# Block 1's inputs, modulated once by side jobs, kept in DRAM and loaded straight into the tiles of their low parts

## The chip, the cores and the metric

The kernel runs on one core of one Trainium2 chip. The core has five engines with a queue of instructions each: TensorE (PE) multiplies matrices and adds into banks (PSUM tiles, named `ps`), ScalarE (ACT) and VectorE (DVE) work on whole tiles, GpSimd (POOL) and SyncE (SP) here do little but issue DMA transfers, which sixteen DMA engines carry out. An engine takes its queue in order; an instruction that waits holds all behind it. The metric is device microseconds (us) from start to end; several runs are timed, and one more execution is recorded by the hardware profiler.

## The reference

One decoder layer on 2048 tokens of width 1024, all in float32. Cut to what matters:

```python
mod = (silu(c) @ w_ada + b_ada)
sh1, sc1, g1, sh2, sc2, g2 = split(mod, 6)
h = x * (1 + sc1) + sh1                          # the modulated input
z = h @ w_in                                     # 1024 -> 2048 columns
gate_b, gate_c, v_conv, v_pool = split(z, 4)
y_conv = gate_b * causal_conv3(gate_c * v_conv)
y_pool = (trailing means over 2, 4, 8, 16 tokens - v_pool) @ w_pool * pool_scale
mix = concat(y_conv, y_pool) @ w_out
x = layer_norm(alpha * x + (1 + g1) * mix)
h = x * (1 + sc2) + sh2
f = square(relu(h @ w_mlp_in)) @ w_mlp_out       # 1024 -> 4096 -> 1024
x = layer_norm(alpha * x + (1 + g2) * f)
```

## The kernel before

**Numbers in two parts.** TensorE multiplies a short form of float32 (`fp32r`). To keep float32's accuracy every operand is cut in two: a high part (ScalarE's cast, L146) and a low part, what the cast lost (VectorE's subtraction, L147). `mm3` (L153 to L155) then issues three matmuls, high by high, high by low, low by high. Weights' parts lie in `w` tiles (6 of them), inputs' parts in `h` tiles (28), what is loaded and not yet cut in `r` tiles (5), intermediate results in `o` tiles (10). Each is 128 x 1024 numbers, 512 KB. A new name for a tile of a kind takes the place of an old one, and the first writer of the new one waits for the last reader of the old.

**Seven products.** The large matrix products are done by Winograd's scheme, two by two blocks with seven products in place of eight. Of the operands some blocks are raw, others sums of blocks. One product (`seven`) has two banks of 12 matmuls, 24 in all; behind its matmuls the code cuts the weights that come next.

**Stages.** Tokens go in two blocks of 1024. Block 0: input projection, output projection and layer norm, then the first MLP matrix (`first_map`) in eight groups `up(b, g)` of 512 hidden columns. Then the same for block 1, and at the end the second MLP matrix for both (`down`). In a group `keep` copies a product's banks into an `o` tile (ScalarE, L1086), `add` adds a product to such a tile, `squared` makes relu and square (ScalarE, L1098 and L1099), and `sums` adds and subtracts quarters of tiles on VectorE, in place, and stores them by POOL's queue into the DRAM tile `usum`. P0 to P6 below are the seven products of block 0's last group, g = 7.

**The turn.** In that group, behind P4, `turn()` calls `prepare()`: it loads what block 1's first input projection needs. The weights `wins` come raw (W0, W1) or summed (from the DRAM tile `winsum`; the first is S below). Inputs are needed raw, that is modulated (key "11" and "21"), or as one of seven sums of blocks (key "2", "1" and on), two tiles each. `summed_weights` loads weights through SyncE's queue (L624). `inputs` loads inputs, also by SyncE (L705): a summed one from the DRAM tile `xsum`, which is then cut by `split`; a raw one from the kernel's input `xT`, whereupon ScalarE modulates it twice, half a tile at a time, once into the `h` tile of the high part and once in place (four instructions of L712 for each tile), and VectorE subtracts for the low part. A program that puts each engine's instructions in order moves all this among P2 to P6 and their sums: the order the engines see is that of the rows shown below, not that of the code.

**Side jobs.** The sums in `xsum` and `winsum` are made earlier. `first_map` calls `beside` behind the products of groups 1 to 7 (a group has seven such calls, one for each product; beats 1 to 5 fall in group 1, 6 to 12 in group 2 and so on, 41 to 47 in group 7). `timed` starts a job at its beat and goes on with it three beats later. `sum_x(k)`, four of them, loads two tiles of `xT` by POOL's queue into two `o` tiles, modulates them (ScalarE), adds and subtracts in place (VectorE) and stores to `xsum`. `sum_first(p)`, two of them, does so with halves of `wins` for `winsum`. POOL's queue has a third kind of traffic: transfers that add w2's blocks to each other in DRAM (`wsum`, L1194), one behind each matmul triple whose number stands in `W_BEATS`.

## Time and profile before

| | |
|---|---|
| median of 3 runs | 1705.73 us (1704.62 to 1708.85) |
| the profiled execution | 1707.25 us |
| its span, first to last instruction | 1705.5 us |
| granted TensorE clock, mean | 0.997 of full speed |
| TensorE busy | 99% of the span |
| VectorE, ScalarE, POOL busy | 82%, 49%, 22% |

The profile is one execution. Its rows name an engine, a line of the code, the operation, and `out<-in` by the tiles' names without their numbers; "x" is a count. A row with square brackets at the end tells how long the engine stood idle before the instruction, and whose end it waited for. In rows of transfers the last figures are sizes and the time from issue to landing. In rows that begin with two times and a colon (a stretch of the span) stand, in this order, its length and the busy us (with the number of instructions) of TensorE, of its weight loads, of VectorE, ScalarE and POOL, then the granted clock, the share of DMA engines' time in use, and GB/s. Groups 1 to 7 of block 0 run from about 313 to 577 us, some 38 us each.

### The profile page before, as it was taken

What the parts mean: (1) busy time and instruction counts of PE and PEld (TensorE: products, weight loads), DVE (VectorE), ACT (ScalarE), POOL (GpSimd) and SP (SyncE); (2) the same over time, 40 slices, a digit from 0 to 9 for tenths busy, and PEclk for the clock granted to TensorE, in tenths of its full rate; (3) what the DMA queues carried; (4) which work ended last, traced back from release to release, by engine and by line L of the source; (5) the groups of instructions that cost most, each with busy time, mean ns of one, the idle gap of its engine ahead of it and who ended that gap; (6) DMA issues with size and microseconds to landing.
All of it is one profiled execution on the core that took longest, in us unless ns stands there. A gap on an engine that the chain in (4) does not pass through costs nothing.

```text
span 1705.5 us, 22025 instructions
## 1 busy us (share of the span) xinstructions
PE 1688.1 (99%) x7519; PEld 1396.8 (82%) x7519; DVE 1399.6 (82%) x2138; ACT 844.2 (49%) x1160; POOL 377.9 (22%) x687
## 2 busy tenths in 40 slices
PE   9999999999999899999999999999999999999998
PEld 7888888888888688888888888888888888888886
DVE  8898697888887586886888788766988887897898
ACT  6323358555554753345855454445543433334555
POOL 0222221445564122200145455430000000000000
PEclk9999999999999999999999999999999999999999
DMA  9998877668778778865889998899899999896782
GB/s 387 346 335 323 312 253 275 224 218 259 241 247 221 228 234 223 238 241 197 267 251 266 243 244 243 240 330 355 317 344 338 384 328 353 292 338 222 264 291 99
DMA packets 149217, 469.47 MB, mean 275 GB/s; under 512 B 20456, under 2 KB 20976, under 8 KB 149104
## 3 DMA queue, kind: packets, MB, share of 16 engines
q1 hardware_dynamic: 93184, 303.38, 50.5%
q0 software_dynamic: 55920, 164.67, 32.0%
q8 instruction: 59, 0.97, 0.3%
q14 instruction: 54, 0.44, 0.1%
HBM read 350.01 MB, written 159.91 MB: 299 GB/s over the span
## 4 chain that ended last, share of the span: by engine, by line
PE 90%; DVE 4%; DMA 3%; ACT 1%; issue 1%; POOL 0%; DVEq 0%; SPq 0%; ACTq 0%; POOLq 0%
PE ps L153 29%; PE ps L155 29%; PE ps L154 29%; PE ps L488 3%; DVE o L164 2%; DMA r<-in_xT 1%; PE ps L865 1%; DMA usum<-o 1%; DVE w L147 1%; DMA w<-in_w 1%; DVE r L164 0%; DMA wsum<-in_w 0%; DMA r<-in_w 0%; POOL usum L1111 0%; ACT w L146 0%
## 5 line engine op out<-in xcount | busy, mean ns | idle before, releaser
L153 PE MATMUL ps<-h,w 128*128 128x512 f32 x1312 | 511.9, 391 | 5.9 <-ACT w L146 4.2
L155 PE MATMUL ps<-h,w 128*128 128x512 f32 x1312 | 511.3, 390 | 0.5 <-DVE w L147 0.5
L154 PE MATMUL ps<-h,w 128*128 128x512 f32 x1312 | 511.7, 390 | 0.0
L153 PE MATMUL ps<-h,h 128*128 128x512 f32 (+1 forms) x1064 | 412.4, 388 | 0.9 <-DVE h L164 0.9
L154 PE MATMUL ps<-h,h 128*128 128x512 f32 (+1 forms) x1064 | 412.4, 388 | 0.9 <-DVE h L147 0.9
L155 PE MATMUL ps<-h,h 128*128 128x512 f32 (+1 forms) x1064 | 412.4, 388 | 0.0
L153 PEld LDWEIGHTS ps<-h,w 128*128 128x128 f32 x1312 | 246.9, 188 | 58.5 <-ACT w L146 4.7
L155 PEld LDWEIGHTS ps<-h,w 128*128 128x128 f32 x1312 | 246.7, 188 | 53.3 <-DVE w L147 1.7
L154 PEld LDWEIGHTS ps<-h,w 128*128 128x128 f32 x1312 | 247.1, 188 | 51.3
L1111 POOL DMA_DIRECT2D usum<-o x416 | 225.2, 550 | 254.2 <-DVE o L164 162.6
L146 ACT CAST w<-r 128x1024 fp32r<-128x1024 f32 x156 | 164.2, 1052 | 196.0 <-PE ps L154 190.4
L147 DVE TENSOR_TENSOR w<-r,w 128x1024 fp32r<-128x1024 f32 x156 | 190.6, 1223 | 59.9 <-ACT w L146 59.1
L146 ACT CAST h<-r 128x1024 fp32r<-128x1024 f32 (+1 forms) x136 | 136.5, 1009 | 198.6 <-PE ps L154 79.6
L154 PEld LDWEIGHTS ps<-h,h 128*128 128x128 f32 x1064 | 199.8, 188 | 42.1 <-DVE h L147 1.3
L153 PEld LDWEIGHTS ps<-h,h 128*128 128x128 f32 x1064 | 199.8, 188 | 42.0 <-DVE h L164 1.1
L155 PEld LDWEIGHTS ps<-h,h 128*128 128x128 f32 x1064 | 199.8, 188 | 40.9
L164 DVE TENSOR_TENSOR o<-o,o 128x256 f32<-128x256 f32 (+2 forms) x458 | 200.7, 491 | 2.7 <-ACT o L1099 1.1
L147 DVE TENSOR_TENSOR h<-r,h 128x1024 fp32r<-128x1024 f32 (+1 forms) x136 | 157.8, 1168 | 51.2 <-ACT h L146 51.0
L146 ACT CAST h<-w 128x1024 fp32r<-128x1024 f32 x104 | 109.1, 1049 | 104.9 <-DVE w L164 95.1
L147 DVE TENSOR_TENSOR h<-w,h 128x1024 fp32r<-128x1024 f32 x104 | 127.1, 1222 | 14.9 <-ACT h L146 14.7
L164 DVE TENSOR_TENSOR o<-o,ps 128x512 f32<-128x512 f32 x184 | 122.7, 684 | 19.2 <-PE ps L155 17.3
L164 DVE TENSOR_TENSOR o<-o 128x256 f32<-128x256 f32 (+1 forms) x176 | 82.6, 472 | 25.3 <-ACT o L1099 14.9
(166 smaller groups left out, 1424.7 us busy)
## 6 DMA issues: line engine op xcount, KB each, us to landing
usum<-o POOLq DMA_DIRECT2D x416, 128.0 KB, 5.2
r<-usum SPq DMA_DIRECT2D x104, 512.0 KB, 5.5
w<-wsum SPq DMA_DIRECT2D x76, 512.0 KB, 7.3
w<-in_w SPq DMA_DIRECT2D x72, 512.0 KB, 7.1
r<-in_w SPq DMA_DIRECT2D x68, 512.0 KB, 7.0
wsum<-in_w POOLq DMA_DIRECT2D x56, 512.0 KB, 7.6
wsum<-wsum POOLq DMA_DIRECT2D x24, 512.0 KB, 5.5
msum<-o POOLq DMA_DIRECT2D x18, 512.0 KB, 6.5
```

Of the source, the lines that this page charges most:

```text
L146: high = nc.scalar.copy(hi, src)
L147: return high.ins, nc.vector.tensor_tensor(lo, src, hi.bitcast(F32), op=ALU.subtract).ins
L153: nc.tensor.matmul(ps, whi, xhi, start=first, stop=False, skip_group_check=goes_on)
L154: nc.tensor.matmul(ps, whi, xlo, start=False, stop=False, skip_group_check=goes_on)
L155: done = nc.tensor.matmul(ps, wlo, xhi, start=False, stop=last, skip_group_check=goes_on)
L164: return nc.vector.tensor_tensor(out_, a, b_, op=op)
L488: nc.tensor.matmul(ps[m, h], wt[:, w : w + P], A[k][p // 2][:, hs], start=k == 0 and p == 0, stop=k == KD - 1 and p == 2)
L865: nc.tensor.transpose(ps[:, t * P : t * P + P], R[4 * h + t][:, k * P : k * P + P], ident)
L1111: nc.gpsimd.dma_start(usum[slot, g // 2, :, b, g % 2, :], z)
```

## The change

There is a new DRAM tile, `xmod`. `sum_x` now stores its two modulated tiles there before it adds in place; it then stops once more, and adds two beats later. So a job holds its two `o` tiles two beats longer. The six jobs start at other beats: 4, 11, 18, 25, 32 and 39 in place of 5, 11, 13, 18, 20 and 26.

`inputs` loads all inputs, raw and summed, from `xmod` or `xsum` without an `r` tile: into the `h` tile of the low part, read as plain float32. `split` then casts from it to the high part, and VectorE subtracts in place. The modulations at L712 are gone: for each raw tile, four modulations of half a tile become one cast of a whole tile.

`inputs` also leaves its last load in the list `fed`, and the next load in `summed_weights` takes it from there: that load is issued behind it (`issue_after` sets an order on the queue, it waits for no data).

```diff
+    xmod = tc.dram_tile([KD, P, T], F32, name="xmod")
...
+    fed = []
+
     def summed_weights(src, sums, order):
         for i in order:
             r = t_r()
-            nc.sync.dma_start(r, src[i] if i in RAW else sums[i - 4])
+            with tc.issue_after(fed.pop()) if fed else nullcontext():
+                nc.sync.dma_start(r, src[i] if i in RAW else sums[i - 4])
             yield r
...
         for i, r in zip((k, k + 4), rs):
             nc.scalar.activation(r, r, AF.Identity, bias=mod[:, 2 * i + SH1 : 2 * i + SH1 + 1],
                                  scale=mod[:, 2 * i + SC1 : 2 * i + SC1 + 1])
+            nc.gpsimd.dma_start(xmod[i], r)
+        yield
         (b11, b12), (b21, b22) = ((r[:, :H], r[:, H:]) for r in rs)
...
         for q in range(2):
-            r = t_r()
             X[key, q] = hi, lo = t_h(), t_h()
...
-                src = xT
-            nc.sync.dma_start(r.rearrange("p (a n) -> p a n", a=2),
-                              src[k : k + 2, :, hs].rearrange("a p n -> p a n"))
-            if len(key) == 1:
-                split(r, hi, lo)
-                continue
-            for dst in (hi, r):
-                for a, cs in enumerate(halves):
-                    nc.scalar.activation(dst[:, cs], r[:, cs], AF.Identity,
-                                         bias=mod[:, 2 * (k + a) + SH1 : 2 * (k + a) + SH1 + 1],
-                                         scale=mod[:, 2 * (k + a) + SC1 : 2 * (k + a) + SC1 + 1])
-            tt(lo, r, hi.bitcast(F32), ALU.subtract)
+                src = xmod
+            r = lo.bitcast(F32)
+            fed[:] = [nc.sync.dma_start(r.rearrange("p (a n) -> p a n", a=2),
+                                        src[k : k + 2, :, hs].rearrange("a p n -> p a n")).ins]
+            split(r, hi, lo)
...
-            for _ in due.pop(beat, ()):
-                pass
+            for job in due.pop(beat, ()):
+                for _ in job:
+                    due.setdefault(beat + 2, []).append(job)
+                    break
             if beat in jobs:
                 next(jobs[beat])
-                due[beat + 3] = jobs[beat]
+                due.setdefault(beat + 3, []).append(jobs[beat])
...
-        return timed(dict(zip((5, 11, 13, 18, 20, 26), sums)))
+        return timed(dict(zip((4, 11, 18, 25, 32, 39), sums)))
```

What the engines see at the turn. In the rows, a name's first number is the tile's own; L624 has become L628, L705 has become L711, L1086 is L1084, L1098 and L1099 are L1096 and L1097. First SyncE's queue before; the row ahead of these is the load of P6's weights (r_657).

```order
L624 DMA r_682_4964<-in_wins 128x1024
L705 DMA r_685_4970<-in_xT 128x2x512
L705 DMA r_688_4979<-in_xT 128x2x512
L705 DMA r_691_4988<-in_xT 128x2x512
L705 DMA r_694_4997<-in_xT 128x2x512
L624 DMA r_697_5006<-in_wins 128x1024
L705 DMA r_700_5012<-xsum_147 128x2x512
L705 DMA r_703_5018<-xsum_147 128x2x512
L624 DMA r_713_5112<-winsum_145 128x1024
```

The weights W0, four raw inputs, the weights W1, two summed inputs, and the first summed weights. Now:

```order
L711 DMA h_686_4980<-xmod_147 128x2x512
L628 DMA r_682_4973<-in_wins 128x1024
L711 DMA h_688_4985<-xmod_147 128x2x512
L711 DMA h_690_4990<-xmod_147 128x2x512
L711 DMA h_692_4995<-xmod_147 128x2x512
L628 DMA r_693_4999<-in_wins 128x1024
L711 DMA h_697_5006<-xsum_148 128x2x512
L711 DMA h_699_5011<-xsum_148 128x2x512
L628 DMA r_707_5103<-winsum_145 128x1024
L711 DMA h_711_5136<-xsum_148 128x2x512
L711 DMA h_713_5141<-xsum_148 128x2x512
```

These loads are called A (h_686), W0 (r_682), B (h_688), C (h_690), D (h_692), W1 (r_693), E (h_697), F (h_699), S (r_707), G (h_711) and H (h_713). A now stands ahead of W0, and the tiles that A to H write were low parts of block 0's inputs: each waits for TensorE's last matmul with the old one. S's `r` tile held the weights of P4 (r_656).

ScalarE in the same place, before. w_676 is the high part of P4's weights, w_679 that of P5's, w_683 that of W0; o_673 takes P2's banks (the copies that free them for P4), o_678 takes P3's, o_664 is P0 and P1's result.

```order
L146 CAST w_676_4911<-r_656_4763 128x1024
L712 ACTIVATE h_686_4971<-r_685_4970,mod_94 128x512
L1098 ACTIVATE o_664_4804<-o_664_4804 128x1024
L712 ACTIVATE h_686_4971<-r_685_4970,mod_94 128x512
L1099 ACTIVATE o_664_4804<-o_664_4804 128x1024
L712 ACTIVATE r_685_4970<-r_685_4970,mod_94 128x512
L1086 COPY o_673_4882<-ps_660_4773 128x512
L146 CAST w_679_4942<-r_655_4762 128x1024
L1086 COPY o_673_4882<-ps_661_4787 128x512
L712 ACTIVATE r_685_4970<-r_685_4970,mod_94 128x512
L712 ACTIVATE h_689_4980<-r_688_4979,mod_94 128x512
L1086 COPY o_678_4915<-ps_674_4885 128x512
```

Two tiles are modulated among the copies, half by half. Now:

```order
L146 CAST h_685_4979<-h_686_4980 128x1024
L146 CAST h_687_4984<-h_688_4985 128x1024
L146 CAST w_676_4920<-r_656_4764 128x1024
L1096 ACTIVATE o_664_4805<-o_664_4805 128x1024
L1097 ACTIVATE o_664_4805<-o_664_4805 128x1024
L146 CAST h_689_4989<-h_690_4990 128x1024
L1084 COPY o_673_4891<-ps_660_4774 128x512
L146 CAST w_679_4951<-r_655_4763 128x1024
L1084 COPY o_673_4891<-ps_661_4788 128x512
L146 CAST h_691_4994<-h_692_4995 128x1024
L1084 COPY o_678_4924<-ps_674_4894 128x512
```

The casts of A and B stand ahead of w_676, that of C ahead of P2's first copy, that of D between the copies.

Then ScalarE up to P6's weights (r_657), before:

```order
L712 ACTIVATE h_692_4989<-r_691_4988,mod_94 128x512 x2
L712 ACTIVATE r_691_4988<-r_691_4988,mod_94 128x512 x2
L712 ACTIVATE h_695_4998<-r_694_4997,mod_94 128x512 x2
L712 ACTIVATE r_694_4997<-r_694_4997,mod_94 128x512
L1098 ACTIVATE o_678_4915<-o_678_4915 128x1024
L712 ACTIVATE r_694_4997<-r_694_4997,mod_94 128x512
L1099 ACTIVATE o_678_4915<-o_678_4915 128x1024
L146 CAST w_698_5008<-r_697_5006 128x1024
L146 CAST h_701_5013<-r_700_5012 128x1024
L146 CAST w_706_5048<-r_657_4764 128x1024
```

and now:

```order
L146 CAST h_696_5005<-h_697_5006 128x1024
L1084 COPY o_678_4924<-ps_675_4907 128x512
L146 CAST w_683_4975<-r_682_4973 128x1024
L146 CAST h_698_5010<-h_699_5011 128x1024
L146 CAST w_694_5001<-r_693_4999 128x1024
L146 CAST h_710_5135<-h_711_5136 128x1024
L1096 ACTIVATE o_678_4924<-o_678_4924 128x1024
L1097 ACTIVATE o_678_4924<-o_678_4924 128x1024
L146 CAST h_712_5140<-h_713_5141 128x1024
L146 CAST w_700_5039<-r_657_4765 128x1024
```

Between W0's cast and P6's (w_706 before, w_700 now) lay eight modulations of half a tile, P3's relu and square, and the casts of W1 and of E; now lie there the casts of F, W1, G and H and the same relu and square, with E's two rows ahead of W0's.

VectorE ahead of the low part of P6's weights, before (the last row):

```order
L147 TENSOR_TENSOR w_699_5009<-r_697_5006,w_698_5008 128x1024
L164 TENSOR_TENSOR o_681_4956<-o_681_4956,o_664_4804 128x256
L164 TENSOR_TENSOR o_681_4956<-o_681_4956,o_678_4915 128x256
L147 TENSOR_TENSOR h_702_5014<-r_700_5012,h_701_5013 128x1024
L147 TENSOR_TENSOR h_705_5020<-r_703_5018,h_704_5019 128x1024
L147 TENSOR_TENSOR w_707_5049<-r_657_4764,w_706_5048 128x1024
```

and now:

```order
L147 TENSOR_TENSOR h_711_5136<-h_711_5136,h_710_5135 128x1024
L164 TENSOR_TENSOR o_673_4891<-o_673_4891,ps_674_4894 128x512
L164 TENSOR_TENSOR o_678_4924<-o_678_4924 128x256
L164 TENSOR_TENSOR o_670_4848<-o_670_4848,o_678_4924 128x256
L164 TENSOR_TENSOR o_670_4848<-o_678_4924,o_664_4805 128x256
L164 TENSOR_TENSOR o_681_4965<-o_664_4805,o_678_4924 128x256
L164 TENSOR_TENSOR o_681_4965<-o_678_4924 128x256
L147 TENSOR_TENSOR h_713_5141<-h_713_5141,h_712_5140 128x1024
L164 TENSOR_TENSOR o_681_4965<-o_681_4965,o_664_4805 128x256
L164 TENSOR_TENSOR o_681_4965<-o_681_4965,o_678_4924 128x256
L147 TENSOR_TENSOR w_701_5040<-r_657_4765,w_700_5039 128x1024
```

The five rows of quarters (128x256) from o_678, which need P3's square, and two more that follow them, stood on both sides of W1's low part (w_699), five ahead of it and outside these rows; now all seven stand behind G's low part and W1's (w_695), with H's among them. P6's low part comes last in both.

TensorE mixes P6's matmuls with those of the input projection's first product, which needs W0, A and B alone. Before, it came to P6's high part after 9 matmuls of that product and to its low part 19 matmuls later; now it comes to the high part after 5 and to the low part 9 later.

## The prediction

> **What bounds the kernel now.** I read the page's head first, then what TensorE waited for, then the stretch round its longest wait engine by engine.
>
> ```profile
> span 1705.5 us, 22025 instructions
> PE 1688.1 (99%) x7519; PEld 1396.8 (82%) x7519; DVE 1399.6 (82%) x2138; ACT 844.2 (49%) x1160; POOL 377.9 (22%) x687
> ...
> PE ps L153 <- ACT w L146: 4.2, 1, 4.2
> PE ps L153 <- ACT o L1086: 1.7, 1, 1.7
> ...
> 560.00:570.00 10.00, 8.35 (x37) 6.53 (x37) 3.91 (x6) 10.00 (x15) 2.13 (x4) 1.00 0.35 107
> 570.00:580.00 10.00, 7.61 (x34) 5.98 (x32) 7.13 (x10) 9.88 (x14) 0.10 (x1) 1.00 0.69 215
> 580.00:590.00 10.00, 8.16 (x24) 6.55 (x25) 7.44 (x11) 4.50 (x5) 3.10 (x6) 0.66 0.93 284
> ```
>
> TensorE is busy for 99% of the span; its two long waits, both on ScalarE, lie in the turn from block 0's last group of products to block 1's input projection. There ScalarE is full (10.00 and 9.88 of 10 us), while before and after it is half idle. The granted clock (the number after POOL's column) falls to 0.66 in the third slice. The matmuls one by one:
>
> ```profile
> 562.32 0.39 PE L155 MATMUL ps<-h,w 128*128 128x512 f32 x1
> 564.36 0.50 PE L153 MATMUL ps<-h,w 128*128 128x512 f32 x1 [1.65 <-ACT o L1086]
> ...
> 577.23 0.39 PE L155 MATMUL ps<-h,w 128*128 128x512 f32 x1
> 581.84 0.80 PE L153 MATMUL ps<-h,w 128*128 128x512 f32 x1 [4.23 <-ACT w L146]
> ...
> 587.55 0.47 PE L153 MATMUL ps<-h,w 128*128 128x512 f32 x1
> 587.86 0.40 PE L154 MATMUL ps<-h,w 128*128 128x512 f32 x1
> ```
>
> From 564.36 to 577.23 there are 57 matmuls, 0.2265 us from start to start. The 14 started from 581.84 until 587.86 take 6.02 us where 14 x 0.2265 = 3.17 would do: the half clock costs 2.85. So the turn loses 1.65 + 4.23 + 2.85 = 8.7 us, which is all this change can win here. Why ScalarE is late:
>
> ```profile
> 551.64 1.05 ACT L146 CAST w<-r 128x1024 fp32r<-128x1024 f32 x1 [3.90 <-PE ps L154]
> 559.72 0.82 ACT L712 ACTIVATE h<-r,mod 128x512 fp32r<-128x512 f32 x1 [7.02 <-DMA r<-in_xT]
> 560.44 1.04 ACT L1098 ACTIVATE o<-o 128x1024 f32<-128x1024 f32 x1
> ...
> 563.74 0.56 ACT L1086 COPY o<-ps 128x512 f32<-128x512 f32 x1
> ...
> 579.80 1.04 ACT L146 CAST h<-r 128x1024 fp32r<-128x1024 f32 x1
> 580.75 1.04 ACT L146 CAST w<-r 128x1024 fp32r<-128x1024 f32 x1
> ...
> L712 ACT ACTIVATE h<-r,mod 128x512 fp32r<-128x512 f32 x8 | 6.3, 808 | 7.1 <-DMA r<-in_xT 7.0
> L712 ACT ACTIVATE r<-r,mod 128x512 f32<-128x512 f32 x8 | 6.2, 806 | 0.0
> ```
>
> ScalarE stands 7.02 us before the first modulation, until its input lands; the copy that frees P4's banks is four instructions behind and ends at 564.30 (first wait). Then come 15 more modulations of 0.71 each, and only at 580.75 the cast of P6's weights, loaded long before (second wait).
>
> **The change part by part.** *ScalarE at the turn.* Before P6's cast, 16 modulations at 0.71 (559.72 to 560.44) = 11.4 us go, and the four tiles get four casts of 0.95 (579.80 to 580.75) = 3.8. The written order also moves four sum-input casts ahead of P6's cast, where there was one: 3 x 0.95 = 2.85. ScalarE thus gains 11.4 - 3.8 - 2.85 = 4.7 us of work. It pays only if the loads are there, so the loads decide.
>
> *The queue of loads.* SyncE's issues before, and where they landed:
>
> ```profile
> 546.63 0.33 SPq L624 DMA_DIRECT2D r<-in_wins  x1
> 548.73 19.38 SPq L705 DMA_DIRECT2D r<-in_xT  x4
> 571.05 0.34 SPq L624 DMA_DIRECT2D r<-in_wins  x1
> ...
> r<-in_wins SPq DMA_DIRECT2D x1, 512.0 KB, 5.0
> ...
> wsum<-in_w POOLq DMA_DIRECT2D x1, 512.0 KB, 10.4
> r<-in_xT SPq DMA_DIRECT2D x1, 512.0 KB, 11.0
> ...
> L705 SPq DMA_DIRECT2D r<-in_xT x2: 378/378/378, 548.7 to 554.0; - x2
> DMA to landing us min/median/max: 7.5/9.2/11.0
> ```
>
> The weights landed at 551.6, the first input at 559.7, the second, issued at 554.0, at 561.5. Now inputs go straight to their low parts' tiles, so what they wait for is no longer an r tile but the last matmul that reads the old tile. P3 ends at 562.55 and a product is 24 x 0.2265 = 5.43, so P0 begins at 540.83. The old low half of A is last read by P0's 17th matmul: A goes at 540.83 + 16 x 0.2265 + 0.39 = 544.9. Then W0 at 546.6 (same wait as before), B at 547, C at 550.3, D at 551.7, W1 behind it, E at 555.7, F at 557.1. That is up to 16 us earlier than the fourth input before (567.7 at latest: 548.73 + 19.38). But they meet the same traffic:
>
> ```profile
> q0 software_dynamic: 237, 0.53, 66.3%
> q1 hardware_dynamic: 201, 0.40, 34.7%
> ...
> q1 hardware_dynamic: 1197, 2.56, 75.9%
> ```
>
> The first two rows are 553 to 557 us, POOL's queue (q0) and SyncE's (q1): with wsum's transfer (10.4 us) running, SyncE's loads got 0.10 MB per us, all engines taken (66.3 + 34.7%). The third is 568 to 579, loads alone: 2.56 MB in 11 us at 75.9% busy, or 0.307 MB per us when fully used, 1.7 us for a load of 0.52 MB and 2.25 at the rate seen. B is third in the queue. Upper bound: the third load before landed at 561.5; lower: 5.0 after issue, as W0 did, 552. I take 560, near the upper end: before, the second in the queue needed until 559.7, and the traffic of POOL is the same. C lands one load later, 562. Behind B come C, D, W1, E, F, S, G: 7 loads at 1.7 to 2.25 are 12 to 16 us, so G lands at 572 to 576 (it stands in SyncE's queue behind S, which waits for P4's low weights until 564, so not before 569.5); POOL's 1.3 MB (four usum of 128 KB, three winsum of 256 KB) lie beside them, so I take 575 and H at 577.
>
> *First wait.* ScalarE's new order is casts of A and B, P4's weights, relu, square, the cast of C, then the copy. From B: 0.95 + 0.95 + 1.05 + 1.05 = 564.0 (C is in by then), the cast 0.95, the copy 0.56: 565.5 against 562.55 wanted. The wait is 3.0 us, 1.4 more than now. It vanishes if B lands by 557.
>
> *Second wait.* These durations of VectorE are used:
>
> ```profile
> 579.52 1.09 DVE L164 TENSOR_TENSOR o<-o,o 128x256 f32<-128x256 f32 x3
> 580.53 0.42 DVE L164 TENSOR_TENSOR o<-o 128x256 f32<-128x256 f32 x1
> 580.86 1.22 DVE L147 TENSOR_TENSOR w<-r,w 128x1024 fp32r<-128x1024 f32 x1
> 582.00 0.76 DVE L164 TENSOR_TENSOR o<-o,o 128x256 f32<-128x256 f32 x2
> ```
>
> That is 0.34 for a quarter-width add and 1.14 for a full low part (580.86 to 582.00). From G at 575 ScalarE does G's cast 0.95, relu 1.1 and square 1.05 (578.1), H's cast 0.95 and P6's cast 0.95 (580.0). VectorE, behind the square: five quarter adds 1.7, H's low part 1.14, two quarter adds 0.7, P6's low part 1.2: 582.8. TensorE reaches P6's high part 48 + 5 matmuls after P4 begins, 565.6 + 12.0 = 577.6, and waits 2.4; nine matmuls more and it stands at 582.0 for P6's low part, and waits 0.8. (Before, the low part came 19 matmuls after the high part, so it had cover; the new order takes that away.) The waits sum to 3.0 + 2.4 + 0.8 = 6.2 against 5.9.
>
> *The clock.* In the trace a wait of 4.23 was followed by the half clock and one of 1.65 was not. 2.4 and 0.8 are nearest 1.65, so they cost 0 more, between bounds of 0 and 2.85. For the first wait of 3.0 it does not matter: the end of the second is set by G, and a slower P4 would only eat from that wait. The Trainium skill (TensorE: Matmul & The Clock Gate, section "What's actually happening") states that the clock falls after a whole free-running window of about 3.4 us without work; both rows agree, and by it none of the new waits costs clock, so its sum is the same as mine and only a single wait of more than 3.4 us, a rival below, would pay.
>
> *Elsewhere.* Eight stores of xmod, 4.2 MB, and four side jobs that hold their two o tiles two beats longer:
>
> ```profile
> xsum<-o POOLq DMA_DIRECT2D x8, 512.0 KB, 6.0
> ...
> 400.00:420.00 20.00, 20.00 (x90) 16.55 (x89) 12.81 (x18) 11.80 (x14) 5.40 (x10) 1.00 0.90 302
> ```
>
> The second xmod store of a job leaves some 7 us after P1 ends (two modulations, relu, square, four usum issues) and lands 6.0 later, at 13; VectorE comes to the first sum that overwrites it 10.9 + 1.8 us after P1's end. So it is held 0 to 1 us, and 5 us where a store takes 10.4 as wsum's did. In 400 to 420 us, where one of these lies, VectorE works 12.81 of 20 us: that slack hides it, and I take 0. If the slack were gone, low parts of weights would come late next. The DMA engines are at 0.90 there; 4.2 MB at 0.307 MB per us is 14 us of them over 200 us, also 0, between 0 and the slower rival's price. The window weights' sums move later, into groups 5 to 7: S, which reads them, waits until 564 anyway, 0; but the second half's four loads now enter POOL's queue near 537, 1.05 MB or 3.4 us of transfers ahead of A. Eight us lie between, so 0 again, between 0 and 3.4 on B. The turns of in-projection products behind P6 wait for nothing that lands after 577 and is wanted before 590: 0.
>
> **The sum.** Now 8.7 us are lost at the turn, then 6.2: 2.5 less. The profiled execution took 1707.25 us (1.75 outside its span) and would take 1704.7; it stands 1.5 above the median, so the median 1705.73 becomes 1703.2. About 0.3%, 5.1 us, is what a measurement of this kernel can tell from no change.
>
> **The rivals.** *Loads come quickly.* If the early issue gets A and B in before wsum's transfer (B by 557, C by 559, G by 569.5, H by 571), only work bounds it. The first wait is 0. VectorE's add of P4's second bank then starts the chain at 570.6: relu, square, H's and P6's casts end at 574.7. VectorE has W1's and G's low parts and P5's first add to do until 573.6, and by the steps above P6's low part ends at 578.3. TensorE wants the high part at 574.6 and the low part 2.0 later: 1.7 of waiting in all. Gain 7.0: 1698.7. For it: W0's 5.0 us and the 14 us of head start; against it: the 10.4 and 11.0 us beside wsum. Chance 0.27.
>
> *One long wait, or none won.* If B comes by 557 but G only at 575, TensorE has no first wait and stands 580.0 - 574.6 = 5.4 in one piece at P6, more than the 4.23 that cost 2.85: in all 5.4 + 2.85 = 8.3, time 1705.3. With B at 560 and G at 578 the first wait is 3.0, P6's cast ends at 583.0, a wait of 5.4, and the half clock follows: 11.3, time 1708.3. This is also the case in which the change moves loads ahead on paper only, because the DMA engines are full. Chance 0.16.
>
> *Slower: the stores hold VectorE.* In each of the four groups with an xmod store VectorE's in-place sum waits until the store lands. Behind it stand the adds that empty TensorE's banks and the low parts. A bank has one product, 5.4 us, of cover, and the add itself takes 0.7: from a store that lands 12.7 + 4.7 us after P1, or 10.4 after its issue, TensorE stands. At 12 us it is 1.6 each and at 14 it is 3.6; with the latter, four times is 14 us, and 1703.2 becomes 1717; with 2 us each, 1711. For it: 10.4 for wsum, 9 to 11 us when POOL's queue is full; against: 6.0 as the median of the xsum stores at this very place. Chance 0.15.
>
> **How the numbers follow.** My forecast, between 1701 and 1705.5, has 0.42, and 1703.2 is its middle. The fast rival ends below 1700.6 (0.3%), the second inside, the slow one above 1710.8. So faster 0.27, same 0.42 + 0.16 = 0.58, slower 0.15. The range of 8 in 10 reaches down to the fast rival's 1698.7 and a little under it, 1698, and up to the mild form of the slow one, 1710.5. What bounds it inside are G's 572 to 576 (3 us) and the clock's 2.85.
>
> **What would show it.** In the profile after: no L712 on ScalarE; inputs' loads issued at 545, 547, 550 and 552 and landing at 5 to 13 us; TensorE's wait for the copy of P2's banks 2 to 4 us near 563 (right) or gone (fast rival); a second wait near 578 of 2 to 3 us on a cast of weights and one of 1 us on a low part (right) or of over 4 us with a granted clock near 0.66 (second rival); no new TensorE wait between 300 and 540 (the slow rival shows there, on VectorE). I am wrong if B lands before 556 or G after 579, if DMA engines give SyncE's loads another share beside wsum than 0.10 MB per us, or if a copy waits for an o tile that a longer side job holds.

## The result, and the profile after

The changed kernel takes 1717.22 us (median of 4 runs, 1715.41 to 1719.16) against 1706.31 for the kernel before (4 runs): 1.0063 times as long, 95% interval 1.0045 to 1.0080. It is slower by 10.9 us; 1703.2 was forecast, with a range up to 1710.5.

What TensorE waited for, in us in total, times, and the longest one:

```profile
PE ps L153 <- ACT o L1084: 5.7, 1, 5.7
PE ps L155 <- DVE w L147: 5.4, 5, 1.7
PE ps L153 <- ACT w L146: 5.1, 1, 5.1
```

The two waits of the turn are both still there and longer (1.65 and 4.23 before); the line between them, on low parts of weights, was 0.5 us in all before. TensorE's matmuls show where it belongs:

```profile
362.04 0.50 PE L155 MATMUL ps<-h,w 128*128 128x512 f32 x1 [1.06 <-DVE w L147]
402.18 0.50 PE L155 MATMUL ps<-h,w 128*128 128x512 f32 x1 [1.73 <-DVE w L147]
...
519.95 0.50 PE L155 MATMUL ps<-h,w 128*128 128x512 f32 x1 [1.36 <-DVE w L147]
...
546.85 0.39 PE L153 MATMUL ps<-h,w 128*128 128x512 f32 x1
...
574.44 0.79 PE L153 MATMUL ps<-h,w 128*128 128x512 f32 x1 [5.67 <-ACT o L1084]
...
577.48 0.39 PE L154 MATMUL ps<-h,w 128*128 128x512 f32 x1
...
593.20 0.79 PE L153 MATMUL ps<-h,w 128*128 128x512 f32 x1 [5.10 <-ACT w L146]
...
597.94 0.40 PE L154 MATMUL ps<-h,w 128*128 128x512 f32 x1
```

Five waits, one in each of groups 2 to 6, always at the third matmul of P2: 5.39 us in all, against one of 0.24 before, or 5.15 more. P0 of group 7 begins at 546.85 in place of 540.78, 6.07 later; that is more than 5.15, because each wait also costs some tenths beside it (behind the wait at 362.04 the next matmul starts after 0.34 us in place of 0.2265). At the turn the waits are 5.67 and 5.10, and after each the clock is half: 7 matmuls from 574.44 to 577.48 take 3.04 where 1.59 would do, 11 from 593.20 to 597.94 take 4.74 where 2.49 would do; 1.45 + 2.25 = 3.70, against 2.85. In sum 5.15 + 4.89 + 0.85 = 10.9 us more, of the 11.9 by which the two profiled spans differ (1717.4 against 1705.5); the tenths beside the waits are most of the rest.

SyncE's issues, and what its queue waited for between 545 and 600 us:

```profile
550.90 0.38 SPq L711 DMA_DIRECT2D h<-xmod  x1
...
554.71 0.33 SPq L628 DMA_DIRECT2D r<-in_wins  x1
555.21 2.85 SPq L711 DMA_DIRECT2D h<-xmod  x3
...
582.30 0.33 SPq L628 DMA_DIRECT2D r<-winsum  x1
```

```profile
SPq L628 <- DMA winsum<-o: 18.7, 1, 18.7
SPq L628 <- DVE w L147: 4.9, 3, 3.4
```

A goes at 550.90, W0 at 554.71 after 3.4 us of waiting for its `r` tile, B at 555.21. S goes only at 582.30: it reads `winsum`, and the side job of beat 39 was still storing it. G and H stand behind S. ScalarE shows what that does:

```profile
558.48 1.05 ACT L146 CAST h<-h 128x1024 fp32r<-128x1024 f32 x1 [4.69 <-DMA h<-xmod]
568.93 1.04 ACT L146 CAST h<-h 128x1024 fp32r<-128x1024 f32 x1 [9.40 <-DMA h<-xmod]
569.88 1.04 ACT L146 CAST w<-r 128x1024 fp32r<-128x1024 f32 x1
...
573.81 0.58 ACT L1084 COPY o<-ps 128x512 f32<-128x512 f32 x1
...
588.17 1.04 ACT L146 CAST h<-h 128x1024 fp32r<-128x1024 f32 x1 [1.62 <-DMA h<-xsum]
...
592.11 1.04 ACT L146 CAST w<-r 128x1024 fp32r<-128x1024 f32 x1
```

It stands 4.69 us for A and 9.40 for B; P4's weights and the copy of P2's banks come behind B. Then G's cast has to wait until 588.17, and P6's weights behind it are cast at 592.11.

### The profile page after: what moved, and what is told of

The parts are those of the page before. It is cut to its first block, busy times and chain, and to the rows that moved or that the text cites. A ratio compares the mean times of both kernels' runs of the same rounds, so it can differ in the third digit from the quotient of the medians.

```text
span 1717.4 us, 22013 instructions
## 1 busy us (share of the span) xinstructions
PE 1689.8 (98%) x7519; PEld 1397.0 (81%) x7519; DVE 1398.9 (81%) x2138; ACT 832.7 (48%) x1142; POOL 382.4 (22%) x695
## 4 chain that ended last, share of the span: by engine, by line
PE 58%; DMA 7%; DVE 5%; issue 2%; POOL 1%; ACT 1%; DVEq 0%; POOLq 0%; SPq 0%; ACTq 0%
PE ps L155 19%; PE ps L153 19%; PE ps L154 19%; DMA usum<-o 3%; DVE o L164 3%; DMA r<-in_w 2%; DMA winsum<-o 1%; DMA wsum<-in_w 1%; DVE w L147 1%; POOL usum L1109 1%; DVE r L164 1%; PE ps L863 0%; DMA wsum<-wsum 0%; DMA h<-xsum 0%; ACT w L146 0%
## 5 line engine op out<-in xcount | busy, mean ns | idle before, releaser
L146 ACT CAST h<-r 128x1024 fp32r<-128x1024 f32 (+1 forms) x128 | 128.1, 1006 | 189.8 <-PE ps L154 76.1
L147 DVE TENSOR_TENSOR h<-r,h 128x1024 fp32r<-128x1024 f32 (+1 forms) x128 | 147.7, 1161 | 48.9 <-ACT h L146 48.6
L147 DVE TENSOR_TENSOR h<-w,h 128x1024 fp32r<-128x1024 f32 x104 | 126.6, 1217 | 12.1 <-ACT h L146 11.9
L1096 ACT ACTIVATE o<-o 128x1024 f32<-128x1024 f32 x48 | 50.9, 1060 | 107.3 <-DVE o L164 107.2
```

The lines of the kernel that those rows point to most:

```text
L146: high = nc.scalar.copy(hi, src)
L147: return high.ins, nc.vector.tensor_tensor(lo, src, hi.bitcast(F32), op=ALU.subtract).ins
L1096: nc.scalar.activation(r, r, AF.Relu)
```

## The experiments

Each kernel below was profiled once and timed. The table adds up what TensorE lost in each profile: "early" are its waits from 340 us to the turn, "first" and "second" those at the turn, "half clock" what slow matmuls behind any of them took beyond 0.2265 us each (to within 0.4 us, by where such a stretch is taken to begin and end). The span less that sum lies between 1696.2 and 1699.1 us in all fourteen, so the sum explains the differences to within three microseconds. Ratios are to the kernel before, run on the same chip.

| kernel | early | first | second | half clock | sum | median | ratio, 95% interval |
|---|---|---|---|---|---|---|---|
| before | 0.2 | 1.7 | 4.2 | 2.9 | 9.0 | | 1 |
| changed | 5.4 | 5.7 | 5.1 | 3.7 | 19.9 | 1717.2 | 1.0063 (1.0045 to 1.0080) |
| late_adds_no_store | 0.6 | 2.2 | 4.1 | 2.6 | 9.4 | 1707.5 | 1.0013 (1.0004 to 1.0023) |
| adds_at_p1 | 8.3 | 6.5 | 3.7 | 7.3 | 25.8 | 1725.0 | 1.0106 (1.0085 to 1.0127) |
| adds_elsewhere | 1.9 | 5.9 | 3.2 | 3.1 | 14.1 | 1713.5 | 1.0048 (1.0030 to 1.0066) |
| xmod_unused | 2.6 | 4.2 | 1.3 | 4.2 | 12.3 | 1712.0 | 1.0046 (1.0028 to 1.0064) |
| winsum_early | 8.7 | 5.1 | 0 | 7.3 | 21.1 | 1717.1 | 1.0067 (1.0052 to 1.0082) |
| wsum_later | 2.7 | 2.9 | 2.5 | 4.5 | 12.7 | 1714.2 | 1.0050 (1.0035 to 1.0065) |
| weights_unordered | 4.2 | 8.2 | 4.2 | 4.3 | 20.9 | 1718.8 | 1.0078 (1.0065 to 1.0090) |
| casts_behind_copies | 4.5 | 0 | 0 | 0 | 4.5 | 1702.3 | 0.9985 (0.9976 to 0.9995) |
| both_mended | 5.0 | 0 | 0 | 2.6 | 7.6 | 1706.3 | 1.0007 (0.9998 to 1.0017) |
| elsewhere_and_behind | 1.1 | 0 | 0 | 0 | 1.1 | 1700.7 | 0.9969 (0.9958 to 0.9979) |
| elsewhere_behind_wsum | 2.0 | 0 | 0 | 0 | 2.0 | 1700.6 | 0.9970 (0.9961 to 0.9980) |
| before_behind | 0.9 | 0 | 0 | 0 | 0.9 | 1699.3 | 0.9964 (0.9950 to 0.9977) |

### The five early waits

The stores of `xmod` and the later place of the adds came together. The first theory was the place: the adds now stand behind P3, among work of which VectorE has none to spare. The rival was the hold: VectorE waits until a store has landed before it may overwrite the tile. In the changed kernel it shows once plainly, in group 2:

```profile
379.01 0.69 DVE L164 TENSOR_TENSOR o<-o 128x512 f32<-128x512 f32 x1 [4.09 <-DMA xmod<-o]
```

**late_adds_no_store**: the changed kernel's side jobs less the store, with `inputs` and `summed_weights` as in the kernel before. Against that kernel:

```diff
             nc.scalar.activation(r, r, AF.Identity, bias=mod[:, 2 * i + SH1 : 2 * i + SH1 + 1],
                                  scale=mod[:, 2 * i + SC1 : 2 * i + SC1 + 1])
+        yield
         (b11, b12), (b21, b22) = ((r[:, :H], r[:, H:]) for r in rs)
...
-        return timed(dict(zip((5, 11, 13, 18, 20, 26), sums)))
+        return timed(dict(zip((4, 11, 18, 25, 32, 39), sums)))
```

(`timed` is the changed kernel's, too.)

> The side jobs of the changed kernel with its beats and its later adds, but without any store of xmod; inputs are loaded and modulated as in the kernel before. 'place': TensorE waits 3.5 to 5.4 us between 360 and 520 us though nothing is stored there; the turn loses about what it lost before (1.65 + 4.23 + 2.85 = 8.7 us), since there the cast of P6's weights does not stand behind the load that follows the first summed weights; time 1709 to 1712. 'hold': under 1 us of waits there; time 1706 to 1708.

The early waits are 0.56 us, the turn loses 8.8 as before, and the time is the one "hold" gave. On VectorE, in the same place as above:

```profile
374.63 0.69 DVE L164 TENSOR_TENSOR o<-o 128x512 f32<-128x512 f32 x1
378.50 1.23 DVE L164 TENSOR_TENSOR r<-r,r 128x1024 f32<-128x1024 f32 x1 [3.19 <-DMA r<-in_w]
379.64 0.68 DVE L164 TENSOR_TENSOR o<-o,o 128x512 f32<-128x512 f32 x1
```

The first add runs at 374.63, the weights' add follows when its load is in, and nothing is lost. So "place" falls: adds of `xsum` there cost 0.3 us, and the rest comes with the stores.

**adds_at_p1**: the changed kernel with the adds back in VectorE's slack, at the same distance from the stores.

```diff
-        return timed(dict(zip((4, 11, 18, 25, 32, 39), sums)))
+        return timed(dict(zip((2, 9, 16, 23, 32, 39), sums)))
```

> The jobs of xmod and xsum start two beats earlier (2, 9, 16, 23), so the adds fall behind P1, where VectorE has slack, and no longer behind P3; the stores of xmod stay two beats ahead of them. Theory 'place' (the five waits of TensorE for a low part of weights between 360 and 520 us, 1.06 + 1.73 + 0.86 + 0.38 + 1.36 = 5.4 us, come from 2.7 us of adds put into a stretch where VectorE has none to spare): the waits fall to under 1.5 us in all, of which the two jobs of winsum, left at their beats, keep a part; the turn stays as it is; time 1712 to 1714. Theory 'hold' (they come from VectorE waiting for the stores of xmod): the distance from store to add is the same, so the waits stay above 3.5 us; time 1716 to 1718.

It became slower still: a miss for both theories in size, and against "place" in kind. VectorE in group 3, then SyncE's loads of the next MLP weights there, and TensorE:

```profile
409.96 0.69 DVE L164 TENSOR_TENSOR o<-o 128x512 f32<-128x512 f32 x1 [5.62 <-DMA xmod<-o]
...
414.77 2.35 DVE L147 TENSOR_TENSOR w<-r,w 128x1024 fp32r<-128x1024 f32 x2
423.38 1.23 DVE L164 TENSOR_TENSOR r<-r,r 128x1024 f32<-128x1024 f32 x1 [6.26 <-DMA r<-in_w]
```

```profile
398.56 17.78 SPq L596 DMA_DIRECT2D r<-in_w  x4
```

```profile
425.26 0.50 PE L153 MATMUL ps<-h,w 128*128 128x512 f32 x1 [2.69 <-DVE o L164]
```

That is the hold's path: VectorE stands 5.62 us for a store, makes two low parts late, and they free the `r` tile of the last of the four loads, which goes out at about 416.3 (398.56 + 17.78); VectorE then stands 6.26 us for it, with the adds that empty TensorE's banks behind. In slack of its own the hold is longer (16.9 us in seven waits, against 6.4 in four); VectorE, with less to do there, probably comes to the adds sooner.

**adds_elsewhere**: the stores stay, but the adds write other tiles and need not wait for them.

```diff
+        to = [t_o() for _ in range(2)]
+        (n11, n12), (n21, n22) = ((r[:, :H], r[:, H:]) for r in to)
-        tt(b12, b12, b11, ALU.subtract)
+        tt(n12, b12, b11, ALU.subtract)
...
-        for i, r in enumerate(rs):
+        for i, r in enumerate(to):
             nc.gpsimd.dma_start(xsum[i, k], r)
```

> The changed kernel, but the adds of xsum write two o tiles of their own, so that they need not wait until the stores of xmod have landed; those stores, and the beats, stay. 'hold' (VectorE stands until the store has landed): the five waits of TensorE between 360 and 520 us, 5.4 us in all, fall under 1.5; turn as in the changed kernel; time 1712 to 1714. 'Full engines' (the 4.2 MB of stores make the loads of MLP weights late, whoever waits for the stores): waits of 3.5 us or more stay; time 1716 to 1718.

1.93 us of early waits are left of 5.39, more than the 1.5 expected, and the time came as "hold" said. That the hold costs time is shown; how much is not sharp. The two pairs of kernels that differ in the place of the adds alone (this one and the changed; elsewhere_and_behind and casts_behind_copies below) differ by 3.5 and 3.4 us of early waits, and their ratios by 0.0015 and 0.0016, which is 2.6 and 2.7 us, with intervals that overlap. But the early waits of one and the same set of side jobs go from 2.6 to 5.4 us in five profiles, and with the adds elsewhere from 1.1 to 2.0 in three. Nor can all five waits of the changed kernel be the hold: the first, 1.06 us at 362.04, comes ahead of the first add that waits for a store (379.01). Ahead of it VectorE had stood for a load of weights until 342.76, where it was 342.07 in the kernel before. What is left above the 0.56 without stores may be the traffic of 4.2 MB; this is not shown.

**xmod_unused**: the changed kernel with all stores, but with the function `inputs` of the kernel before; nobody reads `xmod`.

```diff
-                src = xmod
-            r = lo.bitcast(F32)
...
+            r = t_r()
...
+                src = xT
...
+            for dst in (hi, r):
...
```

> The side jobs of the changed kernel with all their stores of xmod, but inputs are loaded from the kernel's input and modulated at the turn as before; nobody reads xmod. If the waits between 360 and 520 us belong to the stores: 4 to 5.5 us of them, as in the changed kernel, against 0.6 where the same jobs ran without stores; the turn loses about as much as before, 8 to 10 us; time 1710 to 1712. If they belong to something in the new way of loading: under 1 us, time 1706 to 1708.

Early waits of 2.6 us, between the two expectations; its longest, 1.79, is at the place of the 1.73 above. The stores alone do it, without the new way of loading, if less than in the other profile. The turn loses 4.2 + 1.3 and 2.8 of half clock, as much as before.

### The turn

**winsum_early**: the two jobs of `winsum` at beats 9 and 16.

```diff
-        return timed(dict(zip((4, 11, 18, 25, 32, 39), sums)))
+        return timed(dict(zip((4, 11, 18, 25, 9, 16), sums)))
```

> The changed kernel with the two jobs of winsum started at beats 9 and 16 in place of 32 and 39, so that their loads and stores are out of the turn. Theory 'S' (the second wait at the turn, 5.1 us and half clock behind it, comes from SyncE standing 18.7 us before the load S until the last store of winsum has landed, with G and H behind it): S goes at 565 to 572, G lands by 578, the second wait falls under 2.5 us without half clock; the first wait shrinks by 1 to 3 us too, for 2 MB less pass the DMA engines ahead of B; time 1708 to 1711. Theory 'traffic' (DMA engines are full whoever fills them): S goes earlier but G still lands after 584, second wait above 4; time 1714 to 1717.

The second wait is gone, which is "S": SyncE no longer waits for `winsum`. S still goes only at 579.64, not by 572, since its `r` tile now has to be freed by a low part on VectorE (8.1 us of waiting). B stays late, and the first wait is 5.06:

```profile
576.18 1.05 ACT L146 CAST h<-h 128x1024 fp32r<-128x1024 f32 x1 [7.95 <-DMA h<-xmod]
```

The time was missed, since the early waits rose to 8.7 us with 4.5 of half clock. Jobs now overlap, and `o` tiles run out; ScalarE's relu of P6 (L1178) waits for a tile that is still being stored:

```profile
400.76 1.08 ACT L1178 ACTIVATE o<-ps 128x512 f32<-128x512 f32 x2 [5.17 <-DMA usum<-o]
```

**wsum_later**: four transfers of `wsum` moved from just ahead of the turn into block 1.

```diff
-W_BEATS = {44, 62, 79, 109, 123, 166, 209, 282, 291, 327, 338, 348, 369, 377, 386, 395,
+W_BEATS = {44, 62, 79, 109, 123, 166, 209, 282, 291, 327, 338, 348, 501, 507, 513, 519,
```

> The changed kernel with the four transfers of wsum that fall shortly ahead of the turn (numbers 369, 377, 386, 395) moved behind number 500, into block 1. 'Traffic': 2 MB less (and as much again read and written by the adding) ahead of B, which lands by 562 in place of 568.9; first wait under 1 us, 5 us won there; the stores of winsum land earlier as well, by 572, and the second wait falls under 2; time 1707 to 1710. 'S': the first wait shrinks by the same, but the last store of winsum waits for VectorE's adds and lands after 575, so the second wait stays 4 us or more; time 1711 to 1713.

B's cast begins at 565.00, and the first wait falls to 2.94. The second falls to 2.54, between the two expectations: SyncE waits 13.7 us for `winsum` in place of 18.7, so the transfers had held those stores, too. Both theories had expected a first wait under 1 us and at most 1713 us; it took 1714.2. Counted from the start of P0, B's cast begins at +22.1 in the changed kernel, +21.5 with `winsum` early, +22.3 with adds elsewhere and +19.1 here, and the first wait is 5.67, 5.06, 5.91 and 2.94: each is B's time less 16.2 to 16.4. So B's landing sets the first wait, one for one. What fills the engines while B is under way is shown by the share of the DMA engines' time that POOL's queue (q0) and SyncE's (q1) took between 555 and 569 us in the changed kernel, with packets and MB ahead of it:

```profile
q0 software_dynamic: 808, 1.94, 64.4%
q1 hardware_dynamic: 820, 1.85, 41.8%
```

The engines are full; POOL's queue has the larger part of their time, and about half of the bytes. The Trainium skill (DMA: Bandwidth & Descriptors, section "Issuing engines are not separate DMA queues") says that transfers from all queues end up on the same engines and interleave; these rows agree.

**weights_unordered**: the last part of the change undone.

```diff
-            with tc.issue_after(fed.pop()) if fed else nullcontext():
-                nc.sync.dma_start(r, src[i] if i in RAW else sums[i - 4])
+            nc.sync.dma_start(r, src[i] if i in RAW else sums[i - 4])
```

> The changed kernel without its last part, the order of the weights' loads behind the inputs'. SyncE's queue begins A, W0, B as before; then W1 stands ahead of C, and S and the next summed weights ahead of F, so that F and all behind it wait until the last store of winsum has landed. First wait 5 to 6 us, since B is third in either queue; second wait 4.5 to 6.5 us, since P6's cast still stands behind casts whose loads stand behind S. Time 1715 to 1719, the same as the changed kernel. If the order of loads matters, the second wait moves by 3 us or more.

The sum is larger by 1.0, the time by 1.6, inside what was expected; the first wait was missed. It is 8.22, because W1 now goes ahead of C, and C's cast stands ahead of the copy too:

```profile
574.27 1.04 ACT L146 CAST h<-h 128x1024 fp32r<-128x1024 f32 x1 [2.46 <-DMA h<-xmod]
575.22 0.58 ACT L1083 COPY o<-ps 128x512 f32<-128x512 f32 x1
```

So the order of the loads is worth 2.5 us at that copy, and the second wait gives 0.9 of it back.

**casts_behind_copies**: the loads as in the changed kernel, but ScalarE takes the casts of the inputs that the turn loads behind the copies of P3's banks.

```diff
+    held = []
...
             c22 = keep(Z)
+            if g == NC - 1 and b + 1 < NB:
+                held[:] = [mark[0]]
...
-            split(r, hi, lo)
+            with tc.issue_after(held[0]) if held else nullcontext():
+                high = nc.scalar.copy(hi, r)
+            tt(lo, r, hi.bitcast(F32), ALU.subtract)
...
         inputs(X, ORDER[2][1])
+        held.clear()
         return X, W, first_w
```

> The changed kernel, but the casts of the inputs that the turn loads are ordered on ScalarE behind the copies of P3's banks; the loads are as they were. ScalarE's row is then: P4's weights, relu, square, the copies of P2 and P3 with P5's weights and W0, then A, B, relu, square, C, D. TensorE takes P4, P5 and all of the input projection's first product ahead of P6. Theory 'order on ScalarE' (the inputs are early enough for those who need them, and only the copy and P4's weights behind them in the same queue made TensorE wait): both waits at the turn go, 5.7 + 5.1 with 1.0 and 1.6 of half clock, and A's and B's landing at 569 costs nothing; time 1703 to 1706. Theory 'loads' (the inputs themselves are late): TensorE waits 3 us or more for a cast or low part of an input or for S, some 11 to 25 us later than before; time 1709 or more.

Both waits are gone, and it is faster than the kernel before, though only by 0.05 to 0.24%, and a little faster than was expected. ScalarE and the two stretches of the turn (the columns are those of the other stretches):

```profile
562.98 0.58 ACT L1088 COPY o<-ps 128x512 f32<-128x512 f32 x1
...
568.42 0.57 ACT L1088 COPY o<-ps 128x512 f32<-128x512 f32 x1
568.89 2.00 ACT L715 CAST h<-h 128x1024 fp32r<-128x1024 f32 x2
...
583.51 1.05 ACT L146 CAST w<-r 128x1024 fp32r<-128x1024 f32 x1
```

```profile
560.00:580.00 20.00, 20.00 (x90) 16.56 (x89) 12.37 (x21) 9.80 (x12) 7.97 (x15) 1.00 1.04 309
580.00:600.00 20.00, 20.00 (x90) 16.33 (x89) 19.07 (x34) 15.19 (x18) 7.59 (x15) 1.00 1.00 349
```

The DMA engines are as full as ever (1.04), and S still waits 18.5 us for `winsum`; TensorE has 20.00 of 20 us. The inputs were never too late for those who multiply by them, only for the copy behind their casts.

But the edit did more than move casts on ScalarE. The program that puts the engines' instructions in order answered it with another order on TensorE: P6 now begins 76 matmuls after P4 begins, behind all of the input projection's first product, where it began 53 after it in the changed kernel. P4 begins at 567.49 here, and P6's weights are cast from 583.51 to 584.56, 17.1 us later; 76 matmuls take 17.2 us, 53 would take 12.0. So the first wait went by the order on ScalarE, and the second by P6's later place on TensorE: in its old place P6 would still have waited some 5 us (an estimate from these rows). No run moves one without the other.

### Taken together

**both_mended**: adds elsewhere, casts behind the copies, and the jobs of `winsum` at beats 30 and 34 in place of 32 and 39.

> The changed kernel with the adds in tiles of their own, the casts behind the copies, and the two jobs of winsum at beats 30 and 34. If 'hold' and 'order on ScalarE' are both right: under 1.5 us of waits between 360 and 520 and under 2 us at the turn, no half clock; time 1698 to 1702, faster than the kernel before. If o tiles run out (four are held by a job with its adds elsewhere), copies of products wait for one and 3 us or more come back between 340 and 540; time 1703 to 1708.

The turn is clean, the early part is not, for another reason than the one expected. At 519.39 TensorE waits 3.85 us for the low part of P2's weights, and VectorE has this ahead of it:

```profile
514.63 0.69 DVE L164 TENSOR_TENSOR o<-o 128x512 f32<-128x512 f32 x1
...
516.24 1.03 DVE L164 TENSOR_TENSOR o<-o,o 128x512 f32<-128x512 f32 x2
...
517.51 0.69 DVE L164 TENSOR_TENSOR o<-o,o 128x512 f32<-128x512 f32 x1
518.11 1.23 DVE L147 TENSOR_TENSOR w<-r,w 128x1024 fp32r<-128x1024 f32 x1
```

Those half-width adds (128x512) are the `winsum` job's. So a place can probably cost, if it is right ahead of a low part that is due; with the beats put back (next) the wait there is 0.59.

**elsewhere_and_behind**: the same with the beats left at 32 and 39. **elsewhere_behind_wsum**: that, with the four transfers of `wsum` moved as above.

> The changed kernel with the adds of xsum in tiles of their own and the inputs' casts behind the copies of P3's banks; the beats stay at 4, 11, 18, 25, 32 and 39. 'hold' and 'order on ScalarE' together: waits of 1.9 us between 360 and 520 as with the adds elsewhere alone, none at the turn as with the casts behind alone; 2.5 us less than with the casts alone, 1699 to 1701, faster than the kernel before by 0.2 to 0.35%. If a 4 us wait comes near 519 as it did with winsum at beats 30 and 34, it is the tiles held and not those beats: 1703 to 1706.

> The same as adds in tiles of their own with casts behind copies, and the four transfers of wsum numbered 369, 377, 386 and 395 moved into block 1. If traffic at the turn costs nothing once TensorE does not wait there: the same time within 1 us, 1698.5 to 1701. If it still does: 2 us or more are won here, or lost in block 1.

1700.7 and 1700.6: both as expected. The traffic of `wsum`, worth 2.7 us at the first wait while ScalarE's order was bad, is worth nothing once it is good.

**before_behind**: the kernel before, with the modulations ordered behind the copies on ScalarE.

```diff
+                    with tc.issue_after(held[0]) if held else nullcontext():
-                    nc.scalar.activation(dst[:, cs], r[:, cs], AF.Identity, ...)
+                        nc.scalar.activation(dst[:, cs], r[:, cs], AF.Identity, ...)
```

(`held` is set and emptied as above.)

> The kernel before with one edit: the turn's modulations are ordered on ScalarE behind the copies of P3's banks; no xmod, loads and side jobs as they were. 'order on ScalarE' (what was lost at the turn was lost because work for later stood ahead of a copy and of P6's weights): 16 modulations take 11.4 us from 564, the inputs are ready at 568, 572, 575 and 579, TensorE asks for them after P5, from 573 on; waits under 1.5 us, no half clock; 1696.5 to 1699, 0.4 to 0.5% faster than before, and faster than any kernel with xmod. Rival 'input path' (the sixteen modulations and r tiles shared between weights and inputs are the limit whatever the order): W1, whose load waits for an r tile, or D's modulations come 3 us or more late; 1702 to 1706.

```profile
564.17 0.58 ACT L1090 COPY o<-ps 128x512 f32<-128x512 f32 x1
564.65 1.52 ACT L715 ACTIVATE h<-r,mod 128x512 fp32r<-128x512 f32 x2
...
578.82 1.04 ACT L146 CAST w<-r 128x1024 fp32r<-128x1024 f32 x1
```

All sixteen modulations are there, between 564.65 and 578.82, and TensorE waits for none of them; it has one wait of 0.96 us later, at 602.91, for a low part of weights, which the table leaves out. Here, too, P6 has another place on TensorE: 74 matmuls after P4 begins, in place of 57. Its weights are cast behind all the modulations, at 578.82, or 15.6 us after P4 begins at 563.24, hardly earlier than before (580.75 and 564.36, or 16.4); but TensorE asks for them 17 x 0.2265 = 3.9 us later. At 1699.28 us, a little above what was expected, it has the lowest median of all kernels run, 0.23 to 0.50% below the kernel before; its interval overlaps those of the two kernels ahead, so against them it is not told apart, but it needs no `xmod` and no 4.2 MB of stores.

## Why the prediction was wrong

What was right: the three places (the copy, P6's weights, the stores) and the mechanisms at the turn. ScalarE has time there now, and it stands for loads; the lines of waits are the ones named. The rival "the stores hold VectorE", with a chance of 0.15, came true in part: of its 8 to 14 us at most 5.15 came, not all of it by the hold, and the turn did the rest. That the time meets this rival's upper figure, 1717, is chance. The forecast had 6.2 us lost at the turn and nothing new ahead of it; 14.5 were lost there and 5.4 ahead. By its steps:

- *"it is held 0 to 1 us ... that slack hides it, and I take 0"* (early part): 5.15 us, of which the hold is 2.6 to 3.5 by the pairs above; the rest is open. The hold was 4.09 and 0.72 us in group 2. The slack was read as a mean over 20 us, 12.81 busy of 20; but it lies ahead of the add, and what follows the add was full: in the changed kernel VectorE is busy without a gap from 382 to 405, with the low part for the wait at 402.18 in it.
- *"Then W0 at 546.6 (same wait as before), B at 547"* (first wait): counted from P0's start, A was to go at +4.1 and did (550.90 less 546.85). B was to go at +6.2 and land at +19.2; it went at +8.4 and landed at +22.1. Its 13.7 us from issue to landing are near the 13 assumed; the issue was 2.2 us late, because W0, ahead of B in SyncE's queue, waited 3.4 us for a low part on VectorE, where 1.7 were forecast. The first wait was 5.67 in place of 3.0.
- *"S, which reads them, waits until 564 anyway, 0"* (second wait): this step failed outright. It asked when S's tile would be free, and weighed the job's loads as traffic, but not when the data would be there. S waited 18.7 us for the last store of `winsum` and went at 582.30, with G behind it; with `winsum` early the wait vanished. The 564 itself failed, too: P4's low weights, whose cast stands behind B's, are done only at 573. 5.10 in place of 3.2.
- *"so they cost 0 more"* (the clock): 3.70 in place of 0, since both waits grew beyond the 4.23 that had brought it before. Shorter waits bring it too (below): the forecast's own 3.0 would have, and its 2.4 lies between a 2.21 that did not and a 2.54 that did.

These are 5.15 + 2.67 + 1.9 + 3.7 = 13.4 us, the way from 2.5 us faster to 10.9 slower. Beneath them lies one that the prediction had in hand: it listed that A's, B's and C's casts stand ahead of P4's weights and the copy on ScalarE, and took the order as given. The first wait, before and after, was that order, as before_behind and casts_behind_copies show. The second was the place of P6's weights: late in ScalarE's row, and asked for early in TensorE's, which the prediction had counted rightly (53 matmuls after P4) and did not question.

## What to carry to other kernels

An engine's queue that mixes work for later with a copy that frees a bank makes the bank wait for the latest transfer ahead of it; order the work for later behind the copy before spending anything on getting its data sooner, and look at what else the new order moves. A store from a tile that is then overwritten in place is a wait on the computing engine, as long as the store takes to land, and a mean share of busy time doesn't say whether there is slack behind it. Where a producer is moved later, follow its data as well as its buffers: who reads them, and who is queued behind that reader.

## What the runs showed of the hardware

A wait of well under 4 us can bring the half clock, and not always at once. Behind a wait of 2.54 us in wsum_later:

```profile
587.07 0.50 PE L153 MATMUL ps<-h,w 128*128 128x512 f32 x1 [2.54 <-ACT w L146]
587.41 0.45 PE L154 MATMUL ps<-h,w 128*128 128x512 f32 x1
587.66 0.63 PE L153 MATMUL ps<-h,w 128*128 128x512 f32 x1
...
591.05 0.40 PE L153 MATMUL ps<-h,w 128*128 128x512 f32 x1
```

The first two matmuls take 0.59 us from start to start, the next eight 3.39. In the profiles of all kernels here, every wait of 2.5 us or more (19 of them, up to 8.2) was followed by such a stretch, begun within 1.7 us, of 6 to 14 matmuls, 2.7 to 6.1 us, and 1.4 to 2.9 us lost; of the waits between 1.6 and 2.3 us three were (1.79, 1.92 and 2.09) and seven were not (1.60, 1.65, 1.67, 1.73, 2.15, 2.17, 2.21). The prediction drew on the Trainium skill (TensorE: Matmul & The Clock Gate, section "What's actually happening"), by which an idle window of about 3.4 us that runs freely is needed; that it runs freely fits the scattered starts and lengths, the 3.4 us as a least wait does not fit these rows.
